# Small tiles for bias rows and query results, and low parts, sums and scales moved to GpSimd, in a two-layer attention encoder

## The chip, the cores and the metric

The kernel runs on one core of a Trainium2 chip. The time is device microseconds (us) of one execution. A core has five engines that work side by side: TensorE (PE, matrix products, with its weight loads shown apart as PEld), VectorE (DVE), ScalarE (ACT), GpSimd (POOL) and SyncE (SP), which here does nothing but issue transfers (DMAs). Instructions of one engine run in the order in which they stand in its queue, each when the semaphores it waits for have come.

## The reference

Two layers over 1024 tokens of width 1024, in float32. Cut to what matters:

```python
for l in range(2):
    h = rms_norm(x, pre_norm_g[l])
    aq, ak, av, ag, bq, bk, bv, bg = split(h @ w_in[l])      # 512,512,512,512, 512,128,128,512 columns
    lam = exp(sum(lp[0]*lp[1])) - exp(sum(lp[2]*lp[3])) + lam_init
    # group A: 4 heads, two softmaxes each, with a bias by relative position
    sc = einsum('cbhqd,cbhkd->cbhqk', aq*64**-.5, ak) + rel_bias[t5_bucket(kpos - qpos)]
    p = softmax(sc)
    oa = einsum('bhqk,bhkv->bhqv', p[0] - lam*p[1], av)
    ya = rms_norm(oa, diff_subln_g[l]) * (1 - lam_init) * silu(ag)
    # group B: 8 query heads on 2 key heads, normed and rotated by the token's place
    q, k = rope(rms_norm(bq, q_norm_g[l])), rope(rms_norm(bk, k_norm_g[l]))
    yb = (softmax(q*64**-.5 @ k.T) @ bv) * silu(bg)
    x = x + rms_norm(concat([ya, yb]) @ w_out[l], post_norm_g[l])
```

The bias depends on the key's place less the query's alone. So one row of 2047 numbers a head holds it; the kernel makes these rows once, as a product of the table rel_bias with a one-hot matrix of 64 x 2048.

## The kernel before

Every float32 operand of a product is split into a high part (a cast to fp32r) and a low part (the operand less its high part), and a product is three matmuls: high by high, high by low, low by high. The split is two instructions on 128 x 512 or 128 x 1024, the cast mostly on ACT, the subtraction on DVE or POOL.

The tokens are eight tiles of 128. A layer runs these stages:

- **Norm ahead of the projections.** Per token tile a sum of squares (ACT), then row_scale and rpow (line 134): a scale-and-add (tensor_scalar, DVE) and a power of -1/2 (POOL), and products with the result.
- **Projections by token tile** (tok_chunk, line 399): bk and bv, bq, av. A pass is 24 matmuls on 128 x 512. What follows a pass (functions named *_post), and whatever else stands in the list `queue` with a due beat, is run by `follow` after the passes; `beat` counts passes. Line 668 puts the four steps of build_bias_rows there, at the beats of BIAS behind the present one. Weights of the next stage are loaded and converted in the `side` steps of such a chunk.
- **Projections with fewer products** (wino_steps, line 451): ak, ag, bg, aq in four chunks of seven steps n = 0 to 27, two column blocks each; a block is a pass of 12 matmuls on 128 x 512, and counts as a beat. They need sums of weights (t1 to t3 and so on, on DVE) from two loads of each weight block, one into e tiles and one into y tiles (line 477). In the last chunk post_split (line 557) splits the queries' results and store_q (line 564) writes them to DRAM (aq_d), four transfers for each part. The passes of aq that are left over run inside the first steps of attention (FILL).
- **Attention**: four heads by four query groups. Scores go to pS; for group A DVE adds the bias and takes the negated maximum into an e tile, ACT makes the exponentials, POOL joins the two softmaxes; PE transposes into pT, ACT and DVE or POOL split into w tiles, and PE multiplies with the values into pO.
- **End of attention**: in the last steps y_transposed (line 1015) transposes, gates and splits the results of token tiles 0 and 1; then the output projection runs in two halves of 512 columns, y_transposed(t + 2) in the first.
- **Norm and residual** (post_scale, line 1094; residual), and the next layer's norm, in the second half, tile by tile.

Tiles come from rings of buffers: h (10), w (8), e (6, 128 x 1024 floats), y (8, the same size), o (2, 128 x 512); in PSUM pS, pT and pO have two each. An instruction that writes a tile waits until the last reader of that buffer is done, and a transfer out of a tile is such a reader. All transfers go through SP's one queue, in its order.

The order on an engine is the program's where the engine stands in the list `inorder` (in the passes of wino_steps PE alone, line 715; in attention all four); elsewhere a scheduler may move an instruction ahead.

Before, build_bias_rows loads the one-hot matrix into two e tiles of 64 x 1024, rounds each into another e tile, multiplies twice per half (`pl`, a pO bank), copies out into an e tile, and stores to line_d; the second half then issues four copies of 1 MB that repeat a row over 128 partitions (rep_d). Attention reads its bias from rep_d (load_ak, line 684). At n == 21 an exponential of one number (line 737) has ACT load its table for Exp early.

Of the kernel before, what the change touches and what calls it, by code (L numbers as in the profile page):

```python
# [17 lines left out]
P = 128  # L18
# [17 lines left out]
ENDING = (1, 2, 3, 4, 0, 5)  # L36
BIAS = (1, 3, 3, 5)
DUES = (0.5, 1.0, 2.0)
# [15 lines left out]
def hybrid_encoder(ctx, tc, x, rel_bias, pre_norm_g, w_in, diff_lambda, diff_subln_g,  # L54
# [45 lines left out]

    def o_tile(shape=(P, 512)):
        return sb.tile(list(shape), F32, tag="o", name=nm("o"), bufs=2)

# [15 lines left out]
    def f(t):  # L119
        return t.bitcast(F32)  # L120
# [13 lines left out]
    def rpow(dst, src, scale, eps):  # L134
        n = src.shape[-1]
        dve.tensor_scalar(dst, src, scale, eps, ALU.mult, ALU.add)
        gps.tensor_tensor(dst, dst, mhalf[:, :n], ALU.pow)
# [88 lines left out]
    def build_bias_rows():  # L226
# [6 lines left out]
        line_d = d_tile([4, 2048], "line_d")  # L233
        ohs = []
        for j in range(2):
            oh = e_tile()
            nc.sync.dma_start(oh[:64], onehot[:, j * 1024:j * 1024 + 1024])
            ohs.append(oh)

        def rounded(j):  # L240
            oh = e_tile(dt=F32R)
            act.copy(oh[:64], ohs[j][:64])
            ohs[j] = oh

        def line(j):
            lt = e_tile()
            for i in range(2):
                pl = ps_o()
                sl = slice(i * 512, i * 512 + 512)
                pe.matmul(pl[:4], parts, ohs[j][:64, sl], start=True, stop=True)  # L250
                act.activation(lt[:4, sl], pl[:4], AF.Copy, scale=-1.0)
            nc.sync.dma_start(line_d[:, j * 1024:j * 1024 + 1024], lt[:4])
            if j:
                for h in range(4):
                    nc.sync.dma_start(rep_d[h], line_d[h:h + 1, :].broadcast_to([P, 2048]))

        return [lambda: rounded(0), lambda: line(0), lambda: rounded(1), lambda: line(1)]

# [46 lines left out]
    def layer(l, hT, ends, given):  # L305
# [251 lines left out]
        def post_split(cb, th, src):  # L557
            o = e_tile((P, 2, 512), F32R)
            act.copy(o[:, 0], src)
            eng = gps if (cb // 2, th) in ((0, 1), (1, 0)) else dve  # L560
            eng.tensor_tensor(o[:, 1], src, f(o)[:, 0], ALU.subtract)
            store_q(cb, th, f(o))
# [20 lines left out]
        if l == 0:  # L583
# [77 lines left out]
            for t in lates:  # L661
# [4 lines left out]
                                          5: convs[3:]})  # L666
            for i, fn in enumerate(build_bias_rows()):
                queue.append((beat[0] + BIAS[i], fn))
        else:
# [57 lines left out]
        for n in range(7 * len(chunks)):  # L727
# [4 lines left out]
            if n + WPR < len(preps):  # L732
                preps[n + WPR]()
            if n == 21:
                warm = s_tile()
                inorder[:] = [nc.scalar]
                act.activation(warm, neglam, AF.Exp)
                inorder[:] = [nc.tensor]
            if n == 24:
                state["q"], state["ak"], state["bk"] = load_q(0, 0), load_ak(0), load_bk(0)  # L740
                state["bv"] = h_tile([P, 2, NT, P], F32R)
                nc.sync.dma_start(f(state["bv"]), bv_d)
            if n < 7 * len(chunks) - 2:
                for cb in range(2):
# [270 lines left out]
        def y_transposed(t):  # L1015
# [16 lines left out]
            for kh in range(2):  # L1032
                sl = slice(kh * 4, kh * 4 + 4)
                eng = gps if t > 1 else dve
                eng.tensor_tensor(yT[1][:, sl, :], gate[:, sl, :], f(yT[0])[:, sl, :], ALU.subtract)
# [58 lines left out]
        def post_scale(t):  # L1094
            rs_post[t] = s_tile()
            dve.tensor_tensor(rs_post[t], ss[0][t], ss[1][t], ALU.add)
            rpow(rs_post[t], rs_post[t], 1.0 / D, EPS)
# [153 lines left out]
```

## Time and profile before

| what | value |
| --- | --- |
| time, median of 3 runs (lowest to highest) | 1438.78 us (1438.57 to 1438.98) |
| the profiled execution | 1437.0 us |
| its span | 1435.2 us |
| granted TensorE clock, mean | 0.994 |
| PE busy | 1391.2 us (97%), 8108 matmuls |
| PEld busy | 1216.7 us (85%) |
| DVE busy | 1037.9 us (72%), 1824 instructions |
| ACT busy | 836.6 us (58%), 1588 |
| POOL busy | 702.1 us (49%), 740 |
| moved by DMA | 179.12 MB, mean 125 GB/s |

Rows of the timeline read: start, duration, engine, line, operation, tile written <- tiles read, shape, and how many instructions the row joins; in brackets, how long the engine was idle before it and who ended that idleness. Line 67 is a helper that records every operation, so tiles tell them apart. Rows of groups end in busy time, mean ns of one, and idle time before with its releaser. Rows of stretches give start and end, then busy time and instructions of PE, PEld, DVE, ACT and POOL, the granted clock, the busy share of the DMA engines and GB/s.

### The profile page before, as it was taken

Reading aid. Unit: us, or ns where it says so; the run is one execution under the profiler, and the core shown is the slowest. Engines: PE = TensorE matmul, PEld = TensorE weight load, DVE = VectorE, ACT = ScalarE, POOL = GpSimd, SP = SyncE. Lnnn points to the kernel's source line nnn. Section 1 sums busy time; section 2 is a strip of 40 time slices with the busy share of each in tenths; the row PEclk is TensorE's granted clock in tenths of the full one; section 3 lists DMA queues with packets and bytes.
Section 4 is the critical chain, followed back from the end, with each engine's and each line's share of the span. In section 5 each row is a group of like instructions: output and inputs, shape, how many; then the busy total and the mean of one; then the engine's idle time right before and its main releaser. Section 6 shows DMA issues by size and latency. Waiting matters only on the chain.

```text
span 1435.2 us, 22671 instructions
## 1 busy us (share of the span) xinstructions
PE 1391.2 (97%) x8108; PEld 1216.7 (85%) x8108; DVE 1037.9 (72%) x1824; ACT 836.6 (58%) x1588; POOL 702.1 (49%) x740
## 2 busy tenths in 40 slices
PE   6999899989999999989999999999899999999998
PEld 6887788879999999978788888888799999998887
DVE  7878665568888888862686697555688888888423
ACT  5324333458888888853442243343688888888321
POOL 3520000047888888875243200000688888888540
PEclk9999999999999999999999999999999999999999
DMA  6467643474324232142434454337714151222323
GB/s 222 120 165 220 191 148 117 128 236 132 87 67 138 67 82 74 59 147 88 173 111 126 124 162 176 117 110 214 202 56 118 53 146 51 75 89 74 121 71 132
DMA packets 134609, 179.12 MB, mean 125 GB/s; under 512 B 10072, under 2 KB 98392, under 8 KB 132192
## 3 DMA queue, kind: packets, MB, share of 16 engines
q1 hardware_dynamic: 134496, 177.67, 40.8%
q8 instruction: 64, 1.05, 0.3%
q14 instruction: 49, 0.40, 0.1%
HBM read 120.98 MB, written 60.85 MB: 127 GB/s over the span
## 4 chain that ended last, share of the span: by engine, by line
PE 80%; DVE 3%; issue 3%; ACT 2%; DMA 1%; POOL 1%; SPq 0%; DVEq 0%; POOLq 0%; ACTq 0%
PE pO L67 33%; PE pS L67 27%; PE pT L67 20%; DVE y L67 2%; DVE h L67 1%; ACT e L67 1%; POOL e L67 1%; DMA aq_d<-e 1%; DMA y<-in_w_in_dram 1%; ACT w L67 1%; DVE e L67 0%; DVE w L67 0%; ACT o L67 0%; SPq L568 0%; POOL s L67 0%
## 5 line engine op out<-in xcount | busy, mean ns | idle before, releaser
L67 PE MATMUL pO<-w,h 128*128 128x256 f32 (+1 forms) x3160 | 549.2, 321 | 1.0 <-ACT e L67 0.9
L67 PEld LDWEIGHTS pO<-w,h 128*128 128x128 f32 x3160 | 485.3, 189 | 65.3 <-ACT e L67 1.7
L67 PE MATMUL pS<-h,h 128*128 128x512 f32 x1024 | 295.7, 411 | 5.5 <-DVE s L67 3.0
L67 POOL TENSOR_TENSOR e<-y,e 128x512 fp32r<-128x512 f32 x8 | 10.3, 1282 | 399.4 <-DMA h<-aq_d 200.3
L67 PE MATMUL pT<-identr,e 128*128 128x128 f32 x1536 | 201.7, 274 | 3.9 <-DVE w L67 3.8
L67 PEld LDWEIGHTS pS<-h,h 128*128 128x128 f32 x1024 | 175.8, 190 | 30.5 <-DVE s L67 4.4
L67 DVE TENSOR_TENSOR w<-pT,w 128x512 fp32r<-128x512 f32 x256 | 169.9, 685 | 42.2 <-ACT w L67 42.2
L67 PEld LDWEIGHTS pT<-identr,e 128*128 128x128 f32 x1536 | 174.3, 141 | 8.2 <-issue 5.3
L67 POOL TENSOR_TENSOR s<-s,mhalf 128x2 f32<-128x2 f32 (+2 forms) x96 | 84.0, 876 | 185.9 <-DVE s L67 182.5
L67 POOL TENSOR_TENSOR w<-e,w 128x512 fp32r<-128x512 f32 x128 | 165.9, 1296 | 10.4
L67 ACT CAST w<-pT 128x512 fp32r<-128x512 f32 x256 | 143.8, 588 | 38.8 <-PE pT L67 35.8
L67 DVE CUSTOM_DVE_ANT_0 e<-pS,h 128x1024 f32<-128x1024 f32 x128 | 155.6, 1217 | 13.0 <-PE pT L67 5.9
L67 DVE TENSOR_REDUCE s<-pS 128x1 f32<-128x1024 f32 x128 | 156.3, 1221 | 11.5 <-PE pS L67 10.5
L67 ACT ACTIVATE e<-e,s 128x1024 f32<-128x1024 f32 x128 | 148.2, 1158 | 21.8 <-DVE s L67 21.1
L67 POOL TENSOR_TENSOR e<-e,e 128x1024 f32<-128x1024 f32 x64 | 153.2, 2394 | 5.3
L67 ACT ACTIVATE e<-pS,s 128x1024 f32<-128x1024 f32 x128 | 144.6, 1129 | 5.9 <-POOL e L67 5.1
L67 PE MATMUL pT<-h,w 128*128 128x512 f32 x528 | 122.0, 389 | 0.0
L67 PE MATMUL pS<-w,h 128*128 128x512 f32 (+1 forms) x576 | 118.6, 363 | 0.0
L67 PEld LDWEIGHTS pT<-h,w 128*128 128x128 f32 x528 | 99.1, 188 | 20.6
L67 PEld LDWEIGHTS pS<-w,h 128*128 128x128 f32 x576 | 97.2, 195 | 14.6
L67 POOL TENSOR_SCALAR e<-e,s 128x1024 f32<-128x1024 f32 x64 | 72.1, 1127 | 74.1 <-DVE s L67 72.2
L67 ACT ACTIVATE o<-pO 128x128 f32<-128x128 f32 (+2 forms) x97 | 37.0, 382 | 104.8 <-PE pO L67 93.9
(105 smaller groups left out, 1791.0 us busy)
## 6 DMA issues: line engine op xcount, KB each, us to landing
h<-aq_d SPq DMA_DIRECT2D x64, 256.0 KB, 5.0
h<-in_w_in_dram SPq DMA_DIRECT2D x20, 512.0 KB, 4.8
bq_d<-y SPq DMA_DIRECT2D x64, 128.0 KB, 2.4
av_d<-e SPq DMA_DIRECT2D x32, 256.0 KB, 2.4
e<-in_w_in_dram SPq DMA_DIRECT2D x16, 512.0 KB, 4.4
y<-in_w_in_dram SPq DMA_DIRECT2D x16, 512.0 KB, 6.7
ak_d<-e SPq DMA_DIRECT2D x32, 256.0 KB, 2.0
gate_d<-e SPq DMA_DIRECT2D x32, 256.0 KB, 2.0
```

The source lines that it names most:

```text
L67: ins = fn(*args, **kw)
```

## The change

1. The bias rows are made in four pieces of 512 columns. Each piece has two steps: `begun` loads its part of the one-hot matrix into an o tile and rounds it into another, `ended` multiplies once, copies out into an o tile and stores. They are due at the beats of BIAS, `begun` three beats ahead. The four copies to rep_d are issued at the end of the last piece.
2. The queries' results of post_split go to y tiles, and POOL makes the low parts of six of each layer's eight blocks (before, four).
3. The early exponential moves from n == 21 to n == 24; it reads the first query tile, scaled by 0, so it waits for that load.
4. The low part of y_transposed(0) moves from DVE to POOL.
5. The scale-and-add in rpow moves from DVE to POOL everywhere, and so does post_scale's sum.

```diff
-BIAS = (1, 3, 3, 5)
+BIAS = (11, 20, 25, 34)
...
     def rpow(dst, src, scale, eps):
         n = src.shape[-1]
-        dve.tensor_scalar(dst, src, scale, eps, ALU.mult, ALU.add)
+        gps.tensor_scalar(dst, src, scale, eps, ALU.mult, ALU.add)
         gps.tensor_tensor(dst, dst, mhalf[:, :n], ALU.pow)
...
-        ohs = []
-        for j in range(2):
-            oh = e_tile()
-            nc.sync.dma_start(oh[:64], onehot[:, j * 1024:j * 1024 + 1024])
-            ohs.append(oh)
...
-        return [lambda: rounded(0), lambda: line(0), lambda: rounded(1), lambda: line(1)]
+        def piece(j):
+            sl = slice(j * 512, j * 512 + 512)
+            box = []
+
+            def begun():
+                raw_oh = o_tile()
+                nc.sync.dma_start(raw_oh[:64], onehot[:, sl])
+                box.append(o_tile(dt=F32R))
+                act.copy(box[0][:64], raw_oh[:64])
+
+            def ended():
+                pl, lt = ps_o(), o_tile()
+                pe.matmul(pl[:4], parts, box[0][:64], start=True, stop=True)
+                act.activation(lt[:4], pl[:4], AF.Copy, scale=-1.0)
+                nc.sync.dma_start(line_d[:, sl], lt[:4])
+                if j == 3:
+                    for h in range(4):
+                        nc.sync.dma_start(rep_d[h], line_d[h:h + 1, :].broadcast_to([P, 2048]))
+
+            return begun, ended
+
+        return [piece(j) for j in range(4)]
...
         def post_split(cb, th, src):
-            o = e_tile((P, 2, 512), F32R)
+            o = y_tile((P, 2, 512), F32R)
             act.copy(o[:, 0], src)
-            eng = gps if (cb // 2, th) in ((0, 1), (1, 0)) else dve
+            eng = gps if cb > 1 or th else dve
...
-            for i, fn in enumerate(build_bias_rows()):
-                queue.append((beat[0] + BIAS[i], fn))
+            for at, (begun, ended) in zip(BIAS, build_bias_rows()):
+                queue.extend(((beat[0] + at - 3, begun), (beat[0] + at, ended)))
...
-            if n == 21:
-                warm = s_tile()
-                inorder[:] = [nc.scalar]
-                act.activation(warm, neglam, AF.Exp)
-                inorder[:] = [nc.tensor]
             if n == 24:
...
+                act.activation(s_tile(), f(state["q"])[:, :1], AF.Exp, scale=0.0)
...
-                eng = gps if t > 1 else dve
+                eng = dve if t == 1 else gps
                 eng.tensor_tensor(yT[1][:, sl, :], gate[:, sl, :], f(yT[0])[:, sl, :], ALU.subtract)
...
         def post_scale(t):
             rs_post[t] = s_tile()
-            dve.tensor_tensor(rs_post[t], ss[0][t], ss[1][t], ALU.add)
+            gps.tensor_tensor(rs_post[t], ss[0][t], ss[1][t], ALU.add)
```

How the order moves, at three places. First SP's transfers in layer 0 around the first two weight blocks that go to y tiles (e and y from in_w_in_dram are weights, av_d are stores of values, line_d and rep_d the bias rows). Before:

```order
L477 DMA e_1367<-in_w_in_dram 128x4x256
L477 DMA y_1435<-in_w_in_dram 128x4x256
L255 DMA rep_d<-line_d 128x2048 x4
L397 DMA av_d_90<-e_1394 128x4x128 x2
L397 DMA av_d_90<-e_1430 128x4x128 x2
L477 DMA y_1437<-in_w_in_dram 128x4x256
L397 DMA av_d_90<-e_1467 128x4x128 x2
```

Of the change:

```order
L476 DMA e_1339<-in_w_in_dram 128x4x256
L396 DMA av_d_90<-e_1366 128x4x128
L476 DMA y_1407<-in_w_in_dram 128x4x256
L476 DMA y_1409<-in_w_in_dram 128x4x256
L396 DMA av_d_90<-e_1366 128x4x128
L396 DMA av_d_90<-e_1402 128x4x128 x2
L396 DMA av_d_90<-e_1439 128x4x128 x2
L241 DMA o_1626<-in_onehot_dram 64x512
```

The second weight load moves ahead of the value stores, the four copies are gone from this place, and a one-hot piece is loaded behind the stores.

Second, POOL at the start of attention in layer 0, from the first low part of a query block on (e, later y, 128x512 written from y), with the sums and exponentials of group A (e 128x1024) and the splits into w tiles. Before:

```order
L67 TENSOR_TENSOR e_2534<-y_2402,e_2534 128x512
L67 TENSOR_SCALAR e_2499<-e_2499,s_2542 128x1024
L67 TENSOR_TENSOR e_2478<-e_2478,e_2499 128x1024
L67 TENSOR_TENSOR e_2570<-y_2402,e_2570 128x512
L67 CAST w_2497<-e_2531 128x4x128
```

Of the change:

```order
L67 TENSOR_TENSOR y_2447<-y_2294,y_2447 128x512
L67 TENSOR_TENSOR y_2469<-y_2294,y_2469 128x512
L67 TENSOR_TENSOR y_2546<-y_2414,y_2546 128x512
L67 TENSOR_SCALAR e_2511<-e_2511,s_2554 128x1024
L67 TENSOR_TENSOR e_2490<-e_2490,e_2511 128x1024
L67 TENSOR_TENSOR y_2582<-y_2414,y_2582 128x512
L67 CAST w_2509<-e_2543 128x4x128
```

Two low parts come in ahead, and all of them write y tiles in place of e tiles.

Third, DVE at the end of attention in layer 0 (h_6476, later h_6488, holds the gated results of token tiles 0 and 1; h_6814 is the split of tile 0). Before:

```order
L67 SCALAR_TENSOR_TENSOR h_6476<-pT_6815,gsub_665,h_6476 128x4x128
L67 TENSOR_TENSOR h_6476<-pT_6822,h_6476 128x4x128
L67 TENSOR_TENSOR h_6814<-h_6476,h_6814 128x512 x2
L67 TENSOR_TENSOR o_6575<-o_6575,pO_6760 64x256
L67 RECIPROCAL s_6205<-s_6205 128x4
```

Of the change:

```order
L67 SCALAR_TENSOR_TENSOR h_6488<-pT_6827,gsub_665,h_6488 128x4x128
L67 TENSOR_TENSOR h_6488<-pT_6834,h_6488 128x4x128
L67 TENSOR_TENSOR o_6587<-o_6587,pO_6772 64x256
L67 RECIPROCAL s_6217<-s_6217 128x4
```

And POOL at the same place; its w tiles are the last low parts of attention (written from e) and a converted weight of the output projection (from h). Before:

```order
L67 CAST w_6692<-e_6734 128x4x128
L67 TENSOR_TENSOR w_6693<-e_6734,w_6692 128x4x128
L67 TENSOR_TENSOR w_6846<-h_6470,w_6845 128x1024
L67 CAST w_6692<-e_6769 128x4x128
L67 TENSOR_TENSOR w_6693<-e_6769,w_6692 128x4x128
```

Of the change:

```order
L67 CAST w_6704<-e_6746 128x4x128
L67 TENSOR_TENSOR w_6705<-e_6746,w_6704 128x4x128
L67 TENSOR_TENSOR h_6826<-h_6488,h_6826 128x512 x2
L67 TENSOR_TENSOR w_6858<-h_6482,w_6857 128x1024
L67 CAST w_6704<-e_6781 128x4x128
L67 TENSOR_TENSOR w_6705<-e_6781,w_6704 128x4x128
```

The two subtractions leave DVE's place ahead of the sum into the o tile and stand on POOL ahead of the weight and of the last low part.

More of the change, by code (lines that the diff above doesn't have):

```diff
@@ L99, in y_tile, with o_tile @@
         return sb.tile(list(shape), dt, tag="y", name=nm("y"), bufs=8)
-    def o_tile(shape=(P, 512)):
-        return sb.tile(list(shape), F32, tag="o", name=nm("o"), bufs=2)
+    def o_tile(shape=(P, 512), dt=F32):
+        return sb.tile(list(shape), dt, tag="o", name=nm("o"), bufs=2)
     def s_tile(n=1, tag="s", bufs=12):
@@ L233, in build_bias_rows @@
         line_d = d_tile([4, 2048], "line_d")
-        ohs = []
-        for j in range(2):
-            oh = e_tile()
-            nc.sync.dma_start(oh[:64], onehot[:, j * 1024:j * 1024 + 1024])
-            ohs.append(oh)
[L240 to L255, printed above, removed]
-        return [lambda: rounded(0), lambda: line(0), lambda: rounded(1), lambda: line(1)]
+        def piece(j):
[16 more added lines that the diff above has]
+        return [piece(j) for j in range(4)]
     def lambdas(l):
```

## The prediction

> **What bounds the kernel now.** I read the chain of work that ended last first.
>
> ```profile
> PE 80%; DVE 3%; issue 3%; ACT 2%; DMA 1%; POOL 1%; SPq 0%; DVEq 0%; POOLq 0%; ACTq 0%
> ```
>
> TensorE (PE) is the bound: 80% of the chain is its matmuls, and none of them goes away here. What can be won is time in which PE waits, or runs slowly. The table by stretches shows where; columns are length, then busy time (and instructions) of PE, weight loads, DVE, ACT and POOL, the granted PE clock, and DMA.
>
> ```profile
> 20.00:40.00 20.00, 18.15 (x138) 17.34 (x137) 19.47 (x48) 11.06 (x26) 11.92 (x11) 0.91 0.28 96
> ...
> 140.00:160.00 20.00, 15.63 (x67) 12.34 (x66) 9.96 (x9) 7.00 (x9) 0.00 (x0) 0.97 0.79 243
> ...
> 300.00:320.00 20.00, 16.33 (x79) 13.06 (x77) 11.20 (x18) 10.27 (x19) 14.40 (x11) 0.91 0.62 163
> ...
> 620.00:640.00 20.00, 17.54 (x118) 15.07 (x119) 15.28 (x29) 11.20 (x21) 19.22 (x21) 1.00 0.61 207
> ...
> 700.00:760.00 60.00, 56.68 (x322) 47.73 (x321) 50.79 (x103) 24.47 (x53) 22.80 (x23) 1.00 0.37 126
> ...
> 840.00:860.00 20.00, 20.00 (x90) 16.58 (x89) 19.21 (x19) 9.66 (x13) 0.00 (x0) 1.00 0.53 157
> ...
> 1000.00:1020.00 20.00, 16.68 (x83) 13.50 (x82) 11.66 (x19) 12.63 (x24) 11.26 (x9) 0.98 0.67 179
> ```
>
> Five places lose time: the start (20 to 40), the first weight passes of layer 0 (140 to 160; layer 1 at the same place, 840 to 860, loses nothing), the start of attention in both layers (300, 1000), the end of attention (620), the passage between the layers (700 to 760). The change touches all five.
>
> **1. Bias rows, layer 0.** The PE timeline, then three transfer issues and the DVE instruction behind them:
>
> ```profile
> 101.02 5.74 PE L67 MATMUL pO<-w,h 128*128 128x512 f32 x24
> ...
> 106.95 5.74 PE L67 MATMUL pS<-w,h 128*128 128x512 f32 x24
> ...
> 113.89 5.78 PE L67 MATMUL pO<-w,h 128*128 128x512 f32 x24
> 119.50 5.60 PE L67 MATMUL pS<-w,h 128*128 128x512 f32 x24
> 125.04 0.62 PE L67 MATMUL pO<-e,rbs 64*4 64x512 f32 x2
> 126.58 5.75 PE L67 MATMUL pO<-w,h 128*128 128x512 f32 x24 [0.92 <-ACT e L67]
> ...
> 137.60 5.60 PE L67 MATMUL pO<-w,h 128*128 128x512 f32 x24
> 143.04 11.04 PE L67 MATMUL pT<-h,w 128*128 128x512 f32 x48
> 157.87 0.73 PE L67 MATMUL pS<-h,w 128*128 128x512 f32 x2 [3.79 <-ACT w L67]
> ...
> 165.80 4.51 PE L67 MATMUL pS<-w,w 128*128 128x512 f32 x19
> ```
>
> ```profile
> 131.90 0.37 SPq L477 DMA_DIRECT2D y<-in_w_in_dram  x1
> 132.36 2.50 SPq L255 DMA_DIRECT2D rep_d<-line_d  x4
> 134.96 9.85 SPq L397 DMA_DIRECT2D av_d<-e  x4
> 144.87 3.57 SPq L477 DMA_DIRECT2D y<-in_w_in_dram  x1
> ...
> 152.99 1.23 DVE L67 TENSOR_TENSOR y<-y,y 128x1024 f32<-128x1024 f32 x1 [8.44 <-DMA y<-in_w_in_dram]
> ```
>
> A pass of 24 matmuls takes 5.44 (137.60 to 143.04). The second weight load is issued 13 us after the first, behind four 1 MB copies (rep_d) and four stores; DVE waits for it until 152.99, and PE finishes its 48 matmuls at 143.04 + 2 x 5.44 = 153.92 and runs dry. Without that, the pass that starts at 165.80 would start at 153.92 + 5.44 = 159.36: 6.44 lost, slow clock included. The first bias pair delays a pass from the usual step of 5.93 (101.02 to 106.95) to 6.94 (106.95 to 113.89): 1.01. The second costs 126.58 - 119.50 - 5.44 = 1.64. Together 9.09. In the new order both weight loads stand side by side ahead of those stores, and the copies are issued some 60 us later, among the gates' stores, with four of these between them and the next weight loads. Issued at 133, and landing as late as now (8.0 from 144.87 to the DVE), the load is there at 141; four DVE steps of 1.24 and one ACT cast later, near 147, PE's matmuls for it can go, and PE wants them at about 151.6. So the stall goes, and nothing else is late there: layer 1 runs the same passes without the bias at 20.00 of 20. The four matmuls stay, 0.31 each (half of 0.62): 1.24. **Gain 9.1 - 1.2 = 7.9.** Bounds: 5.8, if each of the four single matmuls costs half of what the second pair cost (0.82); 8.2, if they cost 0.23, a pass's matmul. The row nearest to an undisturbed one is 0.31.
>
> **2. Start of attention, twice.** PE, ACT and DVE in layer 0, and stretches of 4 us:
>
> ```profile
> 308.56 1.07 PE L67 MATMUL pS<-h,h 128*128 128x512 f32 x4
> ...
> 310.65 1.22 DVE L67 CUSTOM_DVE_ANT_0 e<-pS,h 128x1024 f32<-128x1024 f32 x1 [2.90 <-PE pT L67]
> ...
> 311.94 1.19 PE L67 MATMUL pS<-h,h 128*128 128x512 f32 x4 [1.43 <-DVE s L67]
> ...
> 315.02 1.35 PE L67 MATMUL pT<-identr,e 128*128 128x128 f32 x8 [1.89 <-DVE w L67]
> ...
> 319.58 1.11 ACT L67 ACTIVATE e<-pS,s 128x1024 f32<-128x1024 f32 x1 [2.58 <-POOL e L67]
> ...
> 320.84 1.18 PE L67 MATMUL pS<-h,h 128*128 128x512 f32 x4 [1.18 <-ACT e L67]
> ```
>
> ```profile
> 312.00:316.00 4.00, 2.11 (x12) 1.44 (x13) 3.40 (x7) 4.00 (x8) 1.30 (x2) 1.00 0.58 148
> 316.00:320.00 4.00, 3.66 (x15) 2.89 (x13) 2.76 (x4) 1.28 (x3) 3.92 (x3) 0.58 0.87 234
> ```
>
> The DVE step at 310.65 has its scores at 309.63 (308.56 + 1.07), but no free e buffer until a query store has landed (the chain runs through such a store there); PE waits 1.43 for it. ACT at 319.58 waits for an e buffer too, and PE 1.18 for ACT. With the queries' results in y tiles the six e buffers serve attention alone: 1.0 of the first wait goes, and the 1.18. The 1.89 stays: ACT is busy 4.00 of 4 there. The clock of 0.58 costs 0.42 x 4 = 1.7; I take half, 0.9, since the idle time ahead of it shrinks by a third and stays near what set it off. On POOL two more units of low parts come in ahead of the exponentials:
>
> ```profile
> L67 POOL TENSOR_TENSOR e<-y,e 128x512 fp32r<-128x512 f32 x8 | 10.3, 1282 | 399.4 <-DMA h<-aq_d 200.3 <-ACT e L67 199.1
> ```
>
> They take 2 x 1.28 in POOL's 200 us of idleness, and DVE loses as many; hidden. The Exp table load moves from the first exponential to a point ahead of it; none of PE's waits above comes from it, so nothing. It now waits for the first query load, with two casts of queries behind it on ACT; the first scores need the same load, so what is late there is late already. If it did hold ACT up, it would show as a wait of PE's for ACT, about 1.2 once more. **1.0 + 1.2 + 0.9 = 3.1, take 3.2 with the rest of the small waits; twice 6.4** (layer 1 has the same loss). Bounds: 0 (POOL's extra 2.6 comes out where the e waits went) and 5.1 per layer.
>
> [...]
>
> **3. End of attention, twice.**
>
> ```profile
> 619.26 1.29 DVE L67 TENSOR_TENSOR h<-h,h 128x512 fp32r<-128x512 f32 x2
> ...
> 621.14 0.41 PE L67 MATMUL pO<-identr,o 128*128 128x128 f32 x2 [1.97 <-DVE o L67]
> ```
>
> ```profile
> L67 POOL TENSOR_TENSOR h<-h,h 128x512 fp32r<-128x512 f32 x24 | 31.2, 1322 | 37.4 <-ACT h L67 37.3
> ```
>
> The 1.29 on DVE stands right ahead of the small sum PE waits for; on POOL it costs 2 x 1.32 = 2.6, in a POOL that is busy 19.22 of 20, and behind it are the last low parts of attention, which PE has yet to multiply. So +1.3 less what comes back, and since PE's wait names DVE's result there and not POOL's, I stay near the upper end: **0.9 each, 1.8** (bounds -1.3, all 2.6 exposed less 1.3, to +1.3).
>
> **4. Scale and sums ahead of the power.** Between the layers:
>
> ```profile
> 726.58 0.15 DVE L67 TENSOR_SCALAR s<-s 128x1 f32<-128x1 f32 x1
> ...
> 727.40 4.61 DVE L67 SCALAR_TENSOR_TENSOR y<-y,s,e 128x1024 f32<-128x1024 f32 x2 [0.67 <-POOL s L67]
> ```
>
> ```profile
> L67 POOL TENSOR_SCALAR s<-s 128x2 f32<-128x2 f32 x32 | 6.2, 193 | 3.0
> ```
>
> DVE idles 0.67 per token tile for a chain that it delays itself: its sum and scale stand behind its product. On POOL they start when ACT is done, cost 0.19 instead of 0.15, and end before that product does. Some 0.7 in each of five tiles is 3.5, as much as PE's idleness from 700 to 760 (60 - 56.68 = 3.3), but DVE works 50.79 of those 60 anyway, so I take a little over half: **1.9** (0 to 3.3). At the start DVE is busy 19.47 of 20 and drops some twelve such steps: **1.0** (0 to 3.6, PE's idle 1.85 plus the clock's 0.09 x 20 = 1.8). The last tile's scale lies on the path to the end: -0.1.
>
> **Sum**: 7.9 + 6.4 + 1.8 + 1.9 + 1.0 - 0.1 = 18.9. The profiled execution took 1437.0 (span 1435.2 and 1.8 around it), so 1418.1; the median shown is 1.8 above it, 1438.8, so **1419.9, say 1420**.
>
> **Rivals.** *POOL and the clock keep the attention starts*: POOL holds DVE up when both work in SBUF. The same small add, twice:
>
> ```profile
> 27.16 1.97 DVE L67 TENSOR_TENSOR y<-y,e 128x128 f32<-128x128 f32 x1
> ...
> 58.54 0.29 DVE L67 TENSOR_TENSOR y<-y,e 128x128 f32<-128x128 f32 x1
> ```
>
> Such an add takes 0.29 at 58.54, so 1.7 was lost at 27.16, beside a POOL operation on 128 x 1024. [...] If this takes away the gains of parts 2 to 4 except the e waits (2 x 2.2 = 4.4), the gain is 7.9 + 4.4 - 1 = 11: 1428. *The change doesn't do what it says* for e buffers (another wait stands right behind): part 2 falls to 1 and the rest stays, 18.9 - 5.4 = 13.5, 1425; together with the first rival, 7.9 + 1 - 1 = 7.9, 1431. *Slower*: the three later one-hot loads stand in the one transfer queue and wait there for PE's previous bias matmul, since there are two o buffers. Weight loads queued behind them would be late: if PE reaches each matmul over 10 us after the queue does, each piece stalls PE as the late load does now, 6.4, three times 19.2 and 1.2 of matmuls against 9.1 + 1 won: some 10 lost, 1449. For it: the queue held such a load for 13 us at 131.90. Against: in the new order each of these loads stands among the stores of results that PE has made just before that matmul, so the queue should come to it hardly earlier than PE.
>
> **Chances.** Forecast (1414 to 1425) 0.58; better, all dips gone, below 1414, 0.12; rivals one and two, alone or together (1425 to 1435) 0.18; nothing to measure 0.05; slower 0.07. The range 1412 to 1432 leaves out about 0.2. A measurement can tell 0.2% from no change (1435.9 to 1441.7): faster 0.87, same 0.06, slower 0.07.
>
> **What would show it.** Right: from 140 to 180 PE busy 20.00 at clock 1.00, no DVE wait for a weight load near 150; no ACT or DVE instruction that waits for an e buffer behind a query store; PE's gap near 620 under 1; DVE's waits for POOL between the layers gone. Wrong: a PE wait at the bias matmuls, POOL named as releaser of PE or DVE near 300 or 625, or a clock under 1 there still.

## The result, and the profile after

The changed kernel takes 1415.59 us (median of 4 runs, 1414.83 to 1416.01) against 1438.88 us before (4 runs, 1438.57 to 1440.37): 23.3 us or 1.6% less, ratio 0.9836 with a 95% interval of 0.9819 to 0.9853. The profiled execution took 1416.0 us (span 1414.3), 21.0 less than that of before. The other 2.3 lie in the two executions chosen: before's profiled one was 1.9 under its median, this one 0.4 over. Ratios, here and below, are of mean times, so they differ a little from those of the medians. Three executions (4942.8 us of e1_bias, 2819.4 of n_halves and 3834.9 of the kernel before) were two to three and a half times as long as all others; they move no median by 0.1 us and are in none of the ratios.

The chain of work of the changed kernel, then its stretches (columns as before):

```profile
PE 91%; POOL 3%; DVE 2%; DMA 2%; ACT 1%; issue 1%; POOLq 0%; DVEq 0%; SPq 0%; ACTq 0%
```

```profile
20.00:40.00 20.00, 17.80 (x146) 16.89 (x144) 18.65 (x41) 11.73 (x27) 14.34 (x19) 1.00 0.31 97
140.00:160.00 20.00, 20.00 (x88) 16.13 (x87) 15.27 (x16) 9.98 (x13) 0.00 (x0) 1.00 0.56 191
300.00:320.00 20.00, 19.75 (x127) 16.25 (x126) 17.04 (x27) 17.05 (x31) 15.26 (x13) 1.00 0.92 236
600.00:620.00 20.00, 16.64 (x126) 15.08 (x125) 15.98 (x28) 13.90 (x30) 19.32 (x18) 0.96 0.39 129
620.00:640.00 20.00, 20.00 (x96) 16.60 (x95) 5.91 (x12) 4.95 (x11) 9.85 (x14) 0.96 0.33 109
700.00:760.00 60.00, 57.23 (x333) 49.04 (x332) 50.23 (x82) 22.91 (x48) 28.84 (x39) 1.00 0.33 101
1000.00:1020.00 20.00, 19.41 (x126) 16.38 (x126) 17.21 (x29) 17.69 (x35) 15.54 (x13) 1.00 1.00 246
```

The passes of layer 0 run without a gap (15.63 busy before, 20.00 now), the start of attention almost without one (16.33 and 16.68 before, 19.75 and 19.41 now), and the clock is whole there. The passage between the layers is little better. The end of attention, now between 600 and 620, waits still and has a clock of 0.96.

Busy time in fixed stretches doesn't say what a stage won, since the work has moved under them. For that I compare the start of the same PE instruction in two traces. Before, these points stand at 54.09 (second pass of the bq projection), 143.04 (first pass of ak), 290.96 (first scores), 617.13 (first transposition of y), 645.60 (the first one in the output projection that is preceded by a whole pass), 733.67 (first projection pass of layer 1), 994.06, 1320.37, 1348.84 (first scores, and the two points at the end of attention, in layer 1) and 1435.2 (end). The table has what each stage won, in us, for the changed kernel and for every kernel with a usable trace, all against that one trace of before; the stage from 733.67 to 994.06 is within 0.1 of 0 in all but two rows (n_late12 -0.3, x_double -0.2).

| kernel | to 54 | to 143 | to 291 | start of attention, layer 0 (to 617) | its end (to 646) | between layers (to 734) | start, layer 1 (994 to 1320) | its end (to 1349) | rest |
| --- | --- | --- | --- | --- | --- | --- | --- | --- | --- |
| forecast | 1.0 | 2.7 | 5.2 | 3.2 | 0.9 | 1.9 | 3.2 | 0.9 | -0.1 |
| changed | 1.6 | 2.8 | 4.3 | 6.1 | -1.0 | 1.1 | 5.5 | 0.6 | 0.0 |
| after_again | 1.8 | 2.8 | 4.3 | 6.0 | -1.0 | 1.1 | 6.2 | 0.5 | 0.0 |
| e1b_bias | 0.1 | 2.8 | 4.3 | -0.3 | 0.2 | 0.0 | 0.1 | 0.0 | 0.2 |
| e2_ytiles | -0.1 | 0.1 | -0.4 | 5.6 | -0.3 | 0.0 | 5.8 | 0.0 | 0.0 |
| e3_sums | 2.2 | 0.0 | -0.8 | -0.1 | 0.0 | 1.1 | 0.1 | -0.4 | -1.1 |
| e4_yt0 | 0.0 | 0.1 | -0.5 | 0.0 | 0.6 | 0.0 | 0.2 | 0.5 | 0.0 |
| m_y0 | 2.1 | 2.8 | 4.3 | 6.0 | 0.0 | 1.1 | 6.2 | 0.0 | 0.1 |
| x_double | 2.1 | 2.8 | 3.4 | 6.0 | 0.5 | 1.1 | 6.2 | 0.6 | 0.0 |
| n_late12 | 2.1 | 2.8 | 4.3 | 6.0 | -0.8 | 1.1 | 6.2 | -0.7 | 0.1 |
| n_halves | 1.8 | 2.8 | 4.3 | 6.0 | -1.6 | 1.1 | 6.2 | -0.1 | 0.0 |
| n_halves_y0 | 2.3 | 2.8 | 4.3 | 6.0 | -0.3 | 1.2 | 5.6 | -0.3 | 0.1 |
| n_halves_split | 2.7 | 2.8 | 4.3 | 6.0 | -1.3 | 1.1 | 6.2 | -1.2 | 0.1 |

Where an edit isn't in a kernel, its column is 0 within 0.3 mostly, with single values to 1.1. Near 155 the clock was at half for 6.8 us in e3_sums and e4_yt0 and for 3.4 in the kernel before (158.97 to 162.38), which goes with the -0.8 and the -0.5; and in e3_sums the last transfer ended 4.2 us after the last VectorE instruction where it took 3.1 before, which makes the -1.1. So a tenth in this table means little, half a microsecond that comes back in several rows means something.

### The profile page after: what moved, and what is told of

Its sections match the earlier page's. It is cut to its first block, busy times and chain, and to the rows that moved or that the text cites. A ratio compares the mean times of both kernels' runs of the same rounds, so it can differ in the third digit from the quotient of the medians.

```text
span 1414.3 us, 22659 instructions
## 1 busy us (share of the span) xinstructions
PE 1385.7 (98%) x8108; PEld 1214.0 (86%) x8108; DVE 1033.3 (73%) x1737; ACT 832.1 (59%) x1586; POOL 724.2 (51%) x827
## 4 chain that ended last, share of the span: by engine, by line
PE 91%; POOL 3%; DVE 2%; DMA 2%; ACT 1%; issue 1%; POOLq 0%; DVEq 0%; SPq 0%; ACTq 0%
PE pO L67 38%; PE pS L67 32%; PE pT L67 21%; POOL w L67 1%; DVE y L67 1%; DMA h<-aq_d 1%; POOL e L67 1%; ACT e L67 1%; POOL h L67 0%; DVE w L67 0%; DMA e<-in_pre_norm_g_dram 0%; DVE h L67 0%; DVE s L67 0%; DMA e<-x_d 0%; ACT w L67 0%
## 5 line engine op out<-in xcount | busy, mean ns | idle before, releaser
L67 POOL TENSOR_TENSOR y<-y,y 128x512 fp32r<-128x512 f32 x12 | 15.5, 1292 | 382.2 <-ACT y L67 192.6
L67 ACT ACTIVATE o<-pO 128x128 f32<-128x128 f32 (+3 forms) x101 | 39.4, 390 | 108.6 <-PE pO L67 107.4
L67 POOL TENSOR_TENSOR s<-s,mhalf 128x2 f32<-128x2 f32 (+2 forms) x96 | 80.0, 834 | 8.0
```

The source lines that it names most:

```text
L67: ins = fn(*args, **kw)
```

## The experiments

### One part of the change at a time

**Bias rows alone**: the kernel before with the new build_bias_rows, BIAS, o_tile and queue lines of the change, and nothing else.

> The kernel before with the bias rows of the change alone (four pieces in o tiles, BIAS 11, 20, 25, 34). Theory: the late weight load was the loss and its going is the whole gain here. The traces of before and after put the gain of this stage at 7.1 us (passes from 113.89 on come 1.0, 1.8 and 4.3 us earlier), since each of the four bias matmuls costs PE 0.5 us and not the 0.3 of the prediction; nothing after it changes, so 1438.9 - 7.1 = 1431.8. Rival: the weight sums on DVE came earlier in the changed kernel because DVE had been freed of the small scales; then the bias rows alone leave a wait near 150 and give 4 us or less, 1435.

The time was 1429.57 us against 1437.67 (8.1 us less, ratio 0.9939, 0.9916 to 0.9962). It ran once more for its trace:

> Once more the kernel before with the bias rows of the change alone, for its trace. Theory: passes 1.0 and 1.8 us earlier by 143 and 4.3 more by the first scores (7.1 in all), weight sums on VectorE that no longer wait near 150, the start of attention unchanged (0 gained there, as e buffers wait as before). Rival: 4 us or less before attention, and some us at its start, since bias tiles no longer take e buffers.

1430.00 against 1438.45 (ratio 0.9940, 0.9917 to 0.9963), and by the table 7.2 us to the first scores and nothing at the start of attention. The theory's 7.1 holds (1437.67 less 7.1 is 1430.6); bias tiles in the e ring cost attention nothing. What the changed kernel's passes look like, PE first, then SP:

```profile
138.66 8.32 PE L67 MATMUL pT<-h,w 128*128 128x512 f32 x36
146.91 0.39 PE L67 MATMUL pO<-o,rbs 64*4 64x512 f32 x1
147.23 3.01 PE L67 MATMUL pT<-h,w 128*128 128x512 f32 x12
150.08 5.60 PE L67 MATMUL pS<-h,w 128*128 128x512 f32 x24
```

```profile
129.10 1.08 SPq L476 DMA_DIRECT2D y<-in_w_in_dram  x2
130.27 10.33 SPq L396 DMA_DIRECT2D av_d<-e  x5
147.33 0.52 SPq L241 DMA_DIRECT2D o<-in_onehot_dram  x1
...
152.00 1.07 SPq L476 DMA_DIRECT2D e<-in_w_in_dram  x2
```

Both weight loads go out at 129.10, and PE runs on from pass to pass. Two passes of 5.44 from 138.66 would end at 149.54; with the one bias matmul the next starts at 150.08, so that matmul costs 0.54 where the prediction had 0.31. The one-hot load at 147.33 goes out when the bias matmul of 146.91 has run, and the weight loads stand behind it until 152.00: this is the wait of the rival that ended slower.

```profile
SPq L241 <- PE pO L67: 11.8, 2, 6.6
```

Line 241 issues the one-hot loads; SP waited for PE there 6.6 us at most, under the 10 from which that rival was to decide, and no PE gap follows.

**y tiles alone**, with the low parts on the engines of before and the early exponential at n == 21:

```diff
         def post_split(cb, th, src):
-            o = e_tile((P, 2, 512), F32R)
+            o = y_tile((P, 2, 512), F32R)
```

> The kernel before with the queries' results in y tiles alone; which engine makes the low parts, and the early exponential, stay as before. Theory: the wait for e buffers behind the query stores was all of the loss at the start of attention, also the 1.89 us wait for DVE that the prediction took to stay; then this alone gives the 6.0 and 5.4 us that the changed kernel gained there, 1438.9 - 11.4 = 1427.5. Rival one: the earlier table load (or one load fewer) and the low parts on GpSimd are needed for half of it: 3 us a layer, 1433. Rival two: with DVE making more of the low parts, the wait of 1.89 for DVE stays and 4 us a layer go: 1431.

1426.78 against 1437.67 (10.9 us less, ratio 0.9919, 0.9900 to 0.9938); 5.6 and 5.8 us in the two layers by the table. One word in one line is half of the whole change. It takes PE's wait of 1.89 for DVE along, which the prediction took to stay since ACT was busy 4.00 of 4 there. Why, ACT's waits in the kernel before show, from 293 to 325, then what it did (columns of the first: in all, times, longest):

```profile
ACT e L67 <- POOL e L67: 6.1, 2, 3.6
...
ACT e L67 <- POOL w L67: 1.2, 1, 1.2
```

```profile
305.33 0.62 ACT L67 CAST e<-y 128x512 fp32r<-128x512 f32 x1 [3.56 <-POOL e L67]
...
309.28 0.62 ACT L67 CAST e<-y 128x512 fp32r<-128x512 f32 x1 [1.22 <-POOL w L67]
...
313.07 0.60 ACT L67 CAST e<-y 128x512 fp32r<-128x512 f32 x1
```

These are casts of query results into e tiles. ACT stood at two of them for 3.56 and 1.22 us, and with them the exponentials and splits behind. The first ended when POOL was done with an e tile of attention's. Attention in turn waits for the stores: the chain of work of the kernel before runs through two of them.

```profile
310.54 2.42 DMA aq_d<-e
...
313.69 2.29 DMA aq_d<-e
315.98 1.12 POOL e L67
```

So ACT was busy 4.00 of 4 from 312 to 316 with work that it had been kept from. With y tiles alone the same work spreads (e2_ytiles, four microseconds a row):

```profile
304.00:308.00 4.00, 4.00 (x23) 3.39 (x22) 2.25 (x3) 2.73 (x5) 3.57 (x4) 1.00 0.42 107
308.00:312.00 4.00, 3.88 (x23) 2.96 (x21) 2.75 (x6) 3.31 (x6) 2.82 (x3) 1.00 0.60 152
312.00:316.00 4.00, 3.92 (x23) 2.85 (x24) 3.87 (x8) 3.75 (x8) 2.95 (x2) 1.00 0.83 191
```

PE is busy 3.9 of 4 all through, and the clock stays at 1.00: without the waits the 0.58 goes too. The earlier table load and the two more low parts on GpSimd come with 0.4 more in layer 0 in all eight kernels that have them, and with 0.4 more in layer 1 in six of the eight; in the changed kernel's own trace PE waits 0.47 for a query load there. They weren't tried by themselves, so what each of them gives stays open below half a microsecond.

**Scale and sums alone** on GpSimd:

```diff
-        dve.tensor_scalar(dst, src, scale, eps, ALU.mult, ALU.add)
+        gps.tensor_scalar(dst, src, scale, eps, ALU.mult, ALU.add)
...
-            dve.tensor_tensor(rs_post[t], ss[0][t], ss[1][t], ALU.add)
+            gps.tensor_tensor(rs_post[t], ss[0][t], ss[1][t], ALU.add)
```

> The kernel before with the scale in rpow and the sum in post_scale on GpSimd alone. Theory: 1.6 us in the prologue and 1.1 us between the layers, as the traces of before and after show, so 1438.9 - 2.7 = 1436.2. Rival: these gains are not of this edit (the passage between the layers begins otherwise after another end of attention); then the prologue's 1.6 remains and the passage gives 0, 1437.3.

1435.89 against 1437.67 (1.8 us less, ratio 0.9980, 0.9962 to 0.9998). The table gives 2.2 in the prologue and 1.1 between the layers, as the theory had it; the late columns of this one execution (-0.8, -0.4 with a drop of the clock, -1.1) aren't in the changed kernel. In the passage DVE's waits for the power fall from 3.1 us in six to 1.3 in three (in all, times, longest; 680 to 765 us before, 670 to 750 in the changed kernel):

```profile
DVE y L67 <- POOL s L67: 3.1, 6, 0.7
```

```profile
DVE y L67 <- POOL s L67: 1.3, 3, 0.6
```

The three that are left were 0.67, 0.66 and 0.67 and are 0.62, 0.20 and 0.49. One of them before, and two in the changed kernel:

```profile
720.08 4.55 DVE L67 SCALAR_TENSOR_TENSOR y<-y,s,e 128x1024 f32<-128x1024 f32 x2 [0.66 <-POOL s L67]
```

```profile
705.16 4.54 DVE L67 SCALAR_TENSOR_TENSOR y<-y,s,e 128x1024 f32<-128x1024 f32 x2 [0.20 <-POOL s L67]
712.54 4.61 DVE L67 SCALAR_TENSOR_TENSOR y<-y,s,e 128x1024 f32<-128x1024 f32 x2 [0.49 <-POOL s L67]
```

At these three places the chain of sum, scale and power, which now starts when ACT is done, still outlasts DVE's work by 0.20 to 0.62 us; the prediction had it end before.

**The low part of the first token tile alone** on GpSimd:

```diff
-                eng = gps if t > 1 else dve
+                eng = dve if t == 1 else gps
```

> The kernel before with the low part of the first token tile of y_transposed on GpSimd alone. Theory: PE's wait for DVE near 621 (1.97 us) falls to 0.5, but GpSimd and VectorE, both at work on two SBUF operands, exclude each other, so that the two subtractions take 3.5 us in place of 2.6 and the weight conversion behind them 3.4 in place of 2.4, and a new wait of PE for GpSimd's last low part (1.3 us) takes most of it back: 0.5 us a layer, 1438. With the low clock that the changed kernel showed in layer 0 behind that wait: -1.0 there and +0.5 in layer 1, 1439.4. Rival: the prediction's 0.9 a layer, 1437.1, with GpSimd's steps at 2.6 and 2.4.

1437.65 against 1437.67 (ratio 0.9995, 0.9985 to 1.0005): no difference in time; 0.6 and 0.5 us in the trace, which such runs can't tell from nothing. What stands in the way shows best in the changed kernel, where the work is the same:

```profile
604.93 0.44 PE L67 MATMUL pO<-identr,o 128*128 128x128 f32 x2 [0.51 <-DVE o L67]
...
608.38 3.50 POOL L67 TENSOR_TENSOR h<-h,h 128x512 fp32r<-128x512 f32 x2
...
608.69 2.06 DVE L67 TENSOR_TENSOR w<-h,w 128x1024 fp32r<-128x1024 f32 x1 [0.87 <-POOL w L67]
...
611.68 1.28 DVE L67 TENSOR_TENSOR w<-h,w 128x1024 fp32r<-128x1024 f32 x1
...
611.84 3.38 POOL L67 TENSOR_TENSOR w<-h,w 128x1024 fp32r<-128x1024 f32 x1
...
617.49 1.29 PE L67 MATMUL pO<-w,h 128*128 128x256 f32 x7 [1.28 <-POOL w L67]
```

PE's wait for the small sum is 0.51, where it was 1.97. But the two moved subtractions take 3.50, not 2.6, and the weight conversion behind them 3.38, not the 2.4 that it takes elsewhere (2.39 at 25.61); the last low part of attention, in the queue behind both, is late by 1.28. In these rows an instruction with two operands in SBUF that began while such a one of the other engine ran took its usual time from where that one ended, to about 0.2 us: DVE's step at 608.69 runs its 1.1 or so after GpSimd's first subtraction ends (608.38 + 1.3 = 609.7) and ends at 610.75; GpSimd's second one starts then and ends at 611.88, 1.1 later. GpSimd's conversion stands until DVE's step of 611.68 ends at 612.96, and ends at 615.22, 2.3 later. DVE's next step, with one operand in PSUM (pT), ran beside that conversion at its usual length (0.74 at 612.88; the 16 of its kind take 0.75 in the mean).

So what the steps moved to GpSimd cost here depended on what DVE did beside them: 3.50 and 3.38, against 2.6 and 2.4.

### The changed kernel again, and without one part

**The changed kernel once more:**

> The changed kernel once more, for the runs beside it. Theory: the 1.0 us that its trace lost at the end of attention in layer 0, where layer 1 won 0.6, came from a drop of the granted clock behind PE's waits that some executions have and others not; so in this trace the two layers differ by the clock alone, and a layer without a drop wins 0.5 to 0.6. Rival: layer 0 loses 1.0 again with the clock at 1.00.

1415.32 against 1437.48 (ratio 0.9839, 0.9821 to 0.9857). Layer 0 lost 1.0 again and layer 1 won 0.5; the clock was under 1 in layer 0 again. x_double below has the same instructions at this place, the same waits, and no drop. The first row is of the changed kernel, the second of x_double:

```profile
616.00:620.00 4.00, 2.72 (x15) 2.52 (x16) 3.70 (x8) 1.72 (x6) 4.00 (x2) 0.78 0.35 114
```

```profile
616.00:620.00 4.00, 2.71 (x20) 2.21 (x19) 3.93 (x7) 2.02 (x7) 3.92 (x3) 1.00 0.27 67
```

Idle as much (2.72 and 2.71 busy), at 0.78 and at 1.00; with the drop the stage lost 1.0, without it it won 0.5. So about 1.5 us there hang on whether a drop comes. The runs say the same: two of the five here had a mean clock of 0.999 and took 1413.3 us, the other three, at 0.997, took 1415.3 to 1417.3. Among the other traces the layout with DVE's long wait drops at times too, at less cost (e2_ytiles in layer 0, a clock of 0.60 from 616 to 620, -0.3; e3_sums in layer 1, 0.84 and 0.74 in the two stretches from 1319.9 to 1327.9, -0.4). The same gaps, then, came with a drop in one execution and without one in another.

The traces also show when it comes. In the kernel before the drops up to 1395 us start at 32.67, 158.97, 315.98 and 1019.12 us, which lie 37, 46 and 206 steps of 3.41 us apart. In each of the 13 traces the drops up to there start on one such grid, and each lasts one step of it (two steps at four places in e3_sums and e4_yt0) at a clock of 0.50. Cut along that grid, the changed kernel's step ahead of its drop and the drop, then x_double's two steps over the same gaps:

```profile
614.80:618.20 3.40, 1.72 (x13) 1.32 (x12) 3.40 (x4) 1.70 (x7) 3.32 (x4) 1.00 0.00 0
618.20:621.60 3.40, 3.40 (x16) 3.00 (x15) 2.35 (x8) 1.60 (x3) 3.40 (x4) 0.50 0.82 255
```

```profile
612.20:615.60 3.40, 3.15 (x26) 2.89 (x26) 3.09 (x4) 1.49 (x3) 3.40 (x3) 1.00 0.19 78
615.60:619.00 3.40, 1.96 (x14) 1.68 (x14) 3.40 (x5) 1.36 (x5) 3.32 (x4) 1.00 0.10 11
```

In the changed kernel two gaps fall into one step, and PE is busy for half of it (1.72 of 3.40); in x_double the same gaps lie otherwise on the grid, and its emptiest step is busy for 0.58. The 13 traces have 5220 such steps at full clock, from where the records of the clock begin (15.61 us in the kernel before, 17.48 in the changed one) up to 1395 us. All 12 in which PE was busy for 0.43 or less were followed by a drop, of the 15 from 0.44 to 0.51 ten were, of the others none. In these traces, then, a drop went with how much of one step was idle, and not with the longest gap: in the kernel before the gap of 1.97 ahead of 621.14 has no drop behind it (its two steps are busy for 0.69 and 0.60), and that of 1.89 ahead of 315.02 has one.

**The low part back on VectorE** (m_y0), all else as changed:

> The changed kernel with the low part of y_transposed(0) back on VectorE. Theory: PE's wait for the small sum is 1.97 again in both layers, the wait for GpSimd's last low part (1.28) is gone; by the trace of that edit alone 0.55 us a layer are lost, 1.1 in all above the changed kernel beside it. Rival: the edit was worth nothing or less, since the wait for GpSimd and the clock behind it cost as much as it gives; then this one is as fast or up to 1 us faster.

1415.08 against 1437.48 (ratio 0.9840, 0.9824 to 0.9856); the changed kernel beside it, 1415.32, is the same. By the trace the end of attention is as before the change (0.0 in both layers). The rival holds as far as the medians can tell: this part of the change is worth nothing that shows. Where no drop came it may be worth its 1.1: at a mean clock of 0.999 the changed kernel took 1413.3 twice, and this one 1414.2 and 1415.2. Four runs are too few to call that shown.

**The low part on VectorE, but later** (n_late12): y_transposed(0) leaves its two subtractions to be issued at the next two steps, behind the small sum.

```diff
-            for kh in range(2):
+            def low(kh):
                 sl = slice(kh * 4, kh * 4 + 4)
-                eng = dve if t == 1 else gps
+                eng = gps if t > 1 else dve
...
+            if t == 0:
+                late_low.extend([lambda: low(0), lambda: low(1)])
...
+            if step in LATE_AT:
+                late_low.pop(0)()
```

LATE_AT is (1, 2).

> The changed kernel with the two subtractions of y_transposed(0) on VectorE, but issued one and two steps later, behind the small sum that PE waits for. Theory: both waits shrink, 1.97 to 0.5 and GpSimd's 1.28 to nothing, since GpSimd has no more to do than before the change: 1.3 us a layer won, 2.6 below the changed kernel beside it. Rival: the subtractions now stand ahead of VectorE's last low parts (PE's wait of 0.61 behind them grows by 0.65 each): 0 to 1 us won.

1416.80 against 1437.48 (ratio 0.9853, 0.9837 to 0.9868), by the trace -0.8 and -0.7 at the two ends. The wait is only moved: PE stands at the next transposition for DVE's low part of attention, which now comes behind the subtractions.

```profile
613.37 1.11 PE L68 MATMUL pT<-identr,y 128*128 128x128 f32 x4 [2.79 <-DVE w L68]
```

The changed kernel waits 0.61 at this place. The rival had named this wait and let it grow by 1.3; it grew by 2.2. So the kernel lost, where the theory had 2.6 us won and the rival 0 to 1.

**Each bias matmul twice:**

```diff
                 pe.matmul(pl[:4], parts, box[0][:64], start=True, stop=True)
+                pe.matmul(pl[:4], parts, box[0][:64], start=True, stop=True)
```

> The changed kernel with each of the four bias matmuls issued twice, the second over the first, so that PE does four more of them. It tells what one of them costs. Theory: 0.53 us is the break in the pass (PE's own weight load for it isn't hidden, and the next pass's first load neither), so a second one right behind costs only its own 0.23 to 0.31, and the passes end 0.9 to 1.2 us later. Rival: every such matmul, on 64 rows and 4 columns, costs 0.53 by itself: 2.1 us later.

1415.09 against 1437.48 (ratio 0.9846, 0.9828 to 0.9863). The column to 291 falls from 4.3 to 3.4: four more matmuls cost 0.9, 0.23 each, as much as one of a pass. The other 0.3 of the 0.53 is the break in the stream, paid once for each piece. PE's weight loads show it; these rows are of x_double, and the changed kernel has the same 0.35 in front of its single one:

```profile
146.33 0.09 PEld L67 LDWEIGHTS pO<-o,rbs 64*4 64x4 f32 x2 [0.35 <-issue]
146.33 0.62 PE L67 MATMUL pO<-o,rbs 64*4 64x512 f32 x2
146.88 2.59 PEld L67 LDWEIGHTS pT<-h,w 128*128 128x128 f32 x12 [0.47 <-ACT w L67]
```

The weight load of the odd matmul starts with it and not ahead of it. The time is no longer than the changed kernel's beside it (1415.32), since this trace has no drop at the end of attention. By these numbers two pieces of two matmuls would cost 1.5 us and four of one cost 2.1: the price of the smaller pieces is 0.6.

### Shorter instructions on GpSimd

**The conversions in halves** (n_halves): GpSimd's low parts of weights as two instructions of 128x512.

```diff
-                eng = dve if (k0 // step + q) in on_dve else gps
-                eng.tensor_tensor(lo[:, sl, :], box[0][:, sl, :], f(hi[:, sl, :]), ALU.subtract)
+                on = (k0 // step + q) in on_dve
+                for i in [sl] if on else [slice(j, j + step // 2) for j in (q * step, q * step + step // 2)]:
+                    (dve if on else gps).tensor_tensor(lo[:, i, :], box[0][:, i, :], f(hi[:, i, :]), ALU.subtract)
```

> The changed kernel with GpSimd's low parts of weights (128x1024, 2.4 us) made in two instructions of 128x512. In the trace of the changed kernel small VectorE sums of two SBUF operands take 1.63 in place of 0.29 while such a GpSimd instruction runs (26.53, 35.85), end when it ends, and PE waits 0.7 and 1.3 behind them. Theory: the two engines exclude each other for a whole instruction; with halves VectorE gets in between, the two sums take 0.7 or less, and the prologue's passes (at 52.5) come 1 to 2 us earlier: 1413.8. Rival: such sums are slowed by GpSimd however long its instruction is; they stay at 1.6 or the second half is held up and the weight comes later: 0, or 0.3 slower from 8 more instructions.

1416.34 against 1438.45 (ratio 0.9838, 0.9817 to 0.9859): no faster. The changed kernel, then this one:

```profile
25.61 2.39 POOL L67 TENSOR_TENSOR w<-h,w 128x1024 fp32r<-128x1024 f32 x1
...
26.53 1.63 DVE L67 TENSOR_TENSOR y<-y,e 128x128 f32<-128x128 f32 x1
...
28.28 1.27 DVE L67 SCALAR_TENSOR_TENSOR y<-y,s,e 128x1024 f32<-128x1024 f32 x1
```

```profile
25.92 2.59 POOL L67 TENSOR_TENSOR w<-h,w 128x512 fp32r<-128x512 f32 x2
...
26.83 0.52 DVE L67 TENSOR_TENSOR y<-y,e 128x128 f32<-128x128 f32 x1
...
27.48 2.11 DVE L67 SCALAR_TENSOR_TENSOR y<-y,s,e 128x1024 f32<-128x1024 f32 x1
```

The mechanism is as the theory had it: the small sum falls from 1.63 to 0.52, since it gets in after the first half. But the product behind it meets the second half and takes 2.11 for 1.27. Of 1.1 us won, 0.8 are gone again two instructions later. The three kernels with halves have 1.8, 2.3 and 2.7 in the prologue's column, those with the changed kernel's code 1.6 to 2.1: some tenths may be won there, but not the 1 to 2 us of the theory. At the end of attention the halves lose, with -1.6 and -0.1 in the two layers where the changed kernel has -1.0 and 0.6; there PE waits for GpSimd once more, for 0.43.

**Halves, and the first tile's low part on VectorE** (n_halves_y0), and **one of its two subtractions on each engine** (n_halves_split, `eng = dve if t == 1 or (t == 0 and kh) else gps`):

> The same, and the low part of y_transposed(0) back on VectorE. Theory: by the last traces the edit on GpSimd gains 0.55 us a layer where the clock holds and loses 1.0 where it drops, and without it the clock held; with the halves nothing changes in that: within 1 us of n_halves, and the end of attention at 0.0 in both layers. Rival: with halves GpSimd's last low part comes early enough in n_halves (its wait of 1.28 goes), and this one is then 1.5 us or more slower than n_halves.

> The same halves, and of the two subtractions of y_transposed(0) one on GpSimd and one on VectorE. Theory: PE's wait for the small sum is 1.3 (between 1.97 and 0.51), GpSimd has 1.3 less to do than in the changed kernel and its last low part no longer is waited for: 0.6 to 0.9 us a layer against the kernel before, no drop of the clock, and so 0 to 1 us faster than n_halves_y0. Rival: VectorE's half is held up by GpSimd's, each waits for the other, and nothing is won.

1415.07 and 1416.62 against 1438.45 (ratios 0.9831, 0.9810 to 0.9852, and 0.9841, 0.9821 to 0.9862). The first is as fast as the changed kernel was beside its own runs of before, and 1.3 us faster than n_halves, a little more than the theory's 1; its end of attention stands at -0.3 in both layers, and not at 0.0. The second wins nothing there (-1.3 and -1.2), and its runs (1415.9 to 1416.9) all lie above those of the first (1414.5 to 1415.7), where the theory had it up to 1 us faster. PE's wait for the small sum is 1.96 still, but not for the rival's reason:

```profile
603.98 0.69 DVE L67 TENSOR_TENSOR h<-h,h 128x512 fp32r<-128x512 f32 x1 [0.69 <-ACT h L67]
```

```profile
607.42 1.28 POOL L67 TENSOR_TENSOR h<-h,h 128x512 fp32r<-128x512 f32 x1
```

VectorE's half takes its usual 0.69, and GpSimd's starts only after it, so neither holds the other up. The half that was left on VectorE is the second one, and it waits 0.69 for ScalarE's cast of the same columns. The small sum behind it starts 3.43 us after the first transposition, as with both halves on VectorE (3.44 before). No version tried is clearly faster than the changed kernel.

## Why the prediction was right, and where its sizes were off

The direction, the place of the gain and the time held: 1415.6 in the range, 1420 forecast, a gain of 23.3 for 18.9 (21.0 between the two traces). That the sum came so near is in part luck, since its errors go both ways: by the changed kernel's row, the starts of attention gave 5.2 more than forecast and the prologue 0.6, and the bias rows, the ends of attention and the passage 3.8 less. Point by point:

- **Bias rows, 7.9 forecast, 7.2 measured.** The late weight load was the larger loss (6.4 of 9.1, the delays by the two bias pairs being the rest), and e1b_bias shows this part of the change alone. The step that was mis-sized is "The four matmuls stay, 0.31 each": a bias matmul costs 0.53, of which 0.23 is the matmul and 0.3 the break, as x_double shows. The first pair of before, at 1.01 for two, had hinted at it. (The 8.0 for the landing is 8.1 by the rows, 144.87 to 152.99, which changes nothing.)
- **Start of attention, 3.2 a layer forecast, 5.5 to 6.2 measured.** The cause was right, shown by y tiles alone (5.6 and 5.8), and the size wrong in two steps. "The 1.89 stays: ACT is busy 4.00 of 4 there" took a busy engine for a bound one: ACT was late from its own waits for e buffers, and with y tiles alone the 1.89 is gone. And of the clock's 1.7 "I take half" left 0.8 out: with the waits the drop went as a whole. The four traces with query results in e tiles have a drop at the start of attention in both layers, the nine with y tiles have none: the gaps went, and so did the dips here. In the step of 3.41 us ahead of the first dip PE is busy 1.51 of 3.40, and the rest of it is the wait of 1.89.
- **End of attention, 0.9 a layer forecast; 0.5 without a drop of the clock, -1.0 with one; nothing in time.** "So +1.3 less what comes back" had the right terms; what came back was larger, since GpSimd's steps took 1.9 us more than by themselves (3.50 and 3.38 against 2.6 and 2.4). The rival with POOL and VectorE in each other's way was at work here, and two of the prediction's signs of being wrong are there: PE waits for POOL (1.28), and the clock is under 1. In the prologue VectorE is held up too (1.63 for a sum of 0.29), but it was so before (1.97), and the forecast gain came.
- **Between the layers, 1.9 forecast, 1.1 measured**: "Some 0.7 in each of five tiles" was too much, as DVE's six waits there were 3.1 in all. And "end before that product does" held for three of DVE's six waits and failed for the others by 0.20 to 0.62. **Prologue, 1.0 forecast, 1.6 to 2.2 measured** without halves, with a spread from run to run as large as the difference. The clock's 1.8 in its upper bound wasn't to be had: e2_ytiles and e4_yt0 have no drop there and win nothing (-0.1 and 0.0).
- **Last tile's scale**, -0.1: the rest column is 0.0 in both traces of the changed kernel.
- **The slower rival** (one-hot loads in the one queue) was there as a wait of up to 6.6 us on SP, without a consequence.

## What to carry to other kernels

A ring of buffers that serves both a store to DRAM and the next stage ties that stage to the store; giving the stored results a ring that is idle at the time was one word here, and half of the gain (5.6 and 5.8 us in the two layers). An engine that is fully busy for a few microseconds is not yet a bound: look whether it waited just ahead, and for what (ACT, busy 4.00 of 4 here, had stood 3.56 us for an e tile). Work moved between VectorE and GpSimd is to be priced with what the other engine does in those microseconds, by instructions and not by shares (here 3.50 and 3.38 for what takes 2.6 and 2.4).

## What the runs showed of the hardware

One bias matmul (64 rows, 4 columns, 512 wide) inside a pass of 24 costs 0.53 us, and a second one right behind it 0.23. In the rows shown, VectorE and GpSimd instructions with two SBUF operands each held the other up until the instruction under way had ended (1.63 for a sum of 0.29 beside one of 2.39, 0.52 beside two of half the size). And the same waits (2.72 and 2.71 busy of 4) came with a granted clock of 0.78 in one execution and 1.00 in another, worth about 1.5 us, which is as much as some of these edits. A step of 3.41 us at half clock came behind every step in which PE was busy for 0.43 or less, and behind none in which it was busy for more than 0.51, in 13 traces.
